# A decoder trunk on one core: low parts of 20 weight blocks formed by GpSimd and an adding transfer in place of VectorE

## The chip, the cores and the metric

The kernel runs on one core of one Trainium2 chip. The metric is the device time of one execution in microseconds. Before the change it was 1330.85 us, the median of three runs (1329.75 to 1331.48).

## The reference

The reference is a trunk of two layers on a sequence of 512 tokens with 1024 features, all in float32. Each layer does the following, cut to what matters here:

```
h = rms_norm(x) * (1 + sc_m) + sh_m
proj = h @ w_in          # 1024 x 3520
x_lru, q_down, kv_down, k_rope, gate_a, gate_b = split(proj)
y_a = rg_lru(conv(x_lru), ...)
y_b = mla(q_down, kv_down, k_rope, ...)        # 8 heads, causal
y = sigmoid(gate_a) * y_a + sigmoid(gate_b) * y_b
x = x + g_m * (y @ w_out)
h = rms_norm(x) * (1 + sc_f) + sh_f
x = x + g_f * ((silu(h @ w_gate) * (h @ w_up)) @ w_ffn_out)
```

The modulation columns sc, sh and g come from a product of the conditioning vector with w_ada (1024 x 6144 in each layer). A last rms_norm ends the trunk.

## The kernel before, in words

Activations lie feature-major: a tile is 128 features by 512 tokens. Each product is made in float32r with operands cut in two: a high part (the value rounded by a copy into float32r) and a low part (value minus high part). Of the four partial products three are made, hi x hi, hi x lo and lo x hi (mm3), so a weight block of 128 output features and 1024 input features takes 24 matmuls of 512 columns: in each group of three, the third one reads the low part of the weight (mm<-hh,wlo).

A weight block is fetched and cut by w_cols. SyncE issues a load of 512 KB into a raw tile; ScalarE copies raw into the tile whi; VectorE subtracts whi from raw into wlo. There are three raw tiles (NRAW) and three pairs of whi and wlo (NHL), which all weights of the kernel share. A raw tile is free again once the low part exists; a pair is free again once the block's 24 matmuls have read it. With dma=True, as before in the last layer's second FFN product alone (fo_block), the low part is made in another way: ScalarE copies whi with scale -1 into wlo, and GpSimd issues a transfer that adds raw to wlo in place.

The first layer begins with first_products, which streams two parts of w_ada and 960 columns of w_in together (x0 to x3 and the down projections). The other 20 blocks of the first layer's w_in go through w_cols: four of x_lru (x4 to x7, called in x_lru through product) and eight each of the two gates (called in gate). The mixer's steps of each layer are listed in SCRIPT: convolution, gates, decay and recurrence of the RG-LRU (x, g, e, w), rope, pairs, scores, transposes and values of the attention (r, p, q, s, t, v), the gates a and b, the merge y, and m, a background step that loads 512 KB of w_ada into a graw tile and reduces it on VectorE. The rotated parts of the queries are put together by 64 small transfers to the tiles stk, issued by SyncE.

No instruction is issued in this textual order. The Recorder collects all calls, and Recorder.order plans them: for each engine it picks the ready call with the longest tail, with modelled durations, modelled latencies between engines, and the limits of the tile pools. Each engine then works through its own list strictly in order. For a transfer issued by GpSimd the plan assumes POOL_DMA ns of issue and POOL_LAT ns more until the data is there; SyncE's loads have constants of their own.

Of the kernel before, what the change touches and what calls it, by code (L numbers as in the profile page):

```python
# [16 lines left out]
AF = mybir.ActivationFunctionType  # L17
ALU = mybir.AluOpType
# [3 lines left out]
P = 128  # L22
# [3 lines left out]
KD = D // P  # L26
# [6 lines left out]
NF = D_FF // P  # L33
# [33 lines left out]
H0, H1, FULL = slice(0, 256), slice(256, 512), slice(0, 512)  # L67
# [38 lines left out]
DMA_RUN = 0.6  # L106
DMA_LAT = 2400.0
DMA_ISSUE = 470.0
POOL_DMA = 1200.0
POOL_LAT = 6000.0  # L110
SHORT = 2000.0
TABLE_LOAD = 1300.0
PE_WINDOW = 3413.0
# [81 lines left out]
class Recorder:  # L195
# [77 lines left out]
    def cost(self, op, eng, method, a, k, outs, ins):  # L273
# [30 lines left out]
        if eng == "POOL":  # L304
            if method == "dma_start":
                return POOL_DMA
            if method == "tensor_scalar":
# [7 lines left out]
    def order(self):  # L315
# [98 lines left out]
        while count < n:  # L414
            for e in ENGINES:
# [62 lines left out]
                end = now + d  # L478
                if e == "POOL" and o.dur == POOL_DMA:
                    end += POOL_LAT  # L480
                if e == "SP":
# [56 lines left out]
def trunk(  # L538
# [7 lines left out]
    V, A, T, G, DMA = (  # L546
        rec.engine(e, r)
        for e, r in (("DVE", nc.vector), ("ACT", nc.scalar), ("PE", nc.tensor), ("POOL", nc.gpsimd), ("SP", nc.sync))
    )
# [12 lines left out]
    def unit(s, dt=F32):  # L562
        return rec.tile(up, [P, 512], dt, "u", NU, nm(s))

    def psum(tag):
        return rec.tile(pp, [P, 512], F32, "ps", BANKS["ps"], nm(tag))
# [7 lines left out]
    def f(ap):  # L574
        return ap.bitcast(F32)

    def split(hi, lo, src):
        A.activation(hi, src, AF.Copy)
        V.tensor_tensor(lo, src, f(hi), ALU.subtract)
# [6 lines left out]
    def mm3(ps, wh, wl, xh, xl, start, stop, **k):  # L586
        T.matmul(ps, wh, xh, start=start, stop=False, **k)
        T.matmul(ps, wh, xl, start=False, stop=False, **k)
        T.matmul(ps, wl, xh, start=False, stop=stop, **k)


    def raw_tile():
        return rec.tile(wp, [P, 1024], F32, "raw", NRAW, nm("raw"))

    def hl_tiles():
        return (
            rec.tile(wp, [P, 1024], F32R, "whi", NHL, nm("whi")),
            rec.tile(wp, [P, 1024], F32R, "wlo", NHL, nm("wlo")),
        )
# [6 lines left out]
            res.append((hi, lo))  # L606
        return res

    def w_cols(src, nk=KD, raws=None, dma=False):


        raw = raw_tile()
        DMA.dma_start(raw[:, : nk * P], src)
        hi, lo = hl_tiles()
        if dma:
            A.activation(hi[:, : nk * P], raw[:, : nk * P], AF.Copy)
            A.activation(lo[:, : nk * P], f(hi[:, : nk * P]), AF.Copy, scale=-1.0)
            G.dma_start(f(lo[:, : nk * P]), raw[:, : nk * P], accum_op=ALU.add)
        else:
            split(hi[:, : nk * P], lo[:, : nk * P], raw[:, : nk * P])  # L620
        if raws is not None:
            raws.extend(raw[:, k * P : (k + 1) * P] for k in range(nk))
        return [(hi[:, k * P : (k + 1) * P], lo[:, k * P : (k + 1) * P]) for k in range(nk)]
# [61 lines left out]
    for i in range(2):  # L685
        ps, crow, cs = psum("pt"), unit("crow"), slice(i * 512, (i + 1) * 512)
# [152 lines left out]
    class Ahead:  # L839
# [12 lines left out]
        def units(self, srcs):  # L852

            raws, res = [], []
            for src in srcs:
                raws.append([])
                w = w_cols(src, raws=raws[-1])
                ps = psum("mm")
                for k, (wh, wl) in enumerate(w):
                    mm3(ps, wh, wl, *self.t[k], k == 0, k == KD - 1)  # L860
                res.append(ps)
            pb, col = psum("o"), small(2 * max(1, NAHEAD), "shc")
            for i in range(len(srcs)):
                a, b = unit("wsa"), unit("wsb")
                for k in range(KD):
                    t = (a if k < 4 else b)[:, (k % 4) * P : (k % 4 + 1) * P]
                    G.tensor_scalar(t, raws[i][k], mcol(self.l, self.ssh, k), 1.0, ALU.mult, ALU.mult)
                G.tensor_tensor(a, a, b, ALU.add)
                G.tensor_tensor(a[:, : 2 * P], a[:, : 2 * P], a[:, 2 * P :], ALU.add)
                G.tensor_tensor(a[:, :P], a[:, :P], a[:, P : 2 * P], ALU.add)  # L870
                T.matmul(pb[:, i : i + 1], a[:, :P], ones[:, :1], start=True, stop=True)
            V.tensor_copy(col[:, : len(srcs)], pb[:, : len(srcs)])
            return res, [col[:, i : i + 1] for i in range(len(srcs))]


    def w_quarters(srcs):

        raws = []
        for src in srcs:
            raw = raw_tile()  # L880
            DMA.dma_start(raw, src)
            raws.append(raw)
        lo_, hi_ = slice(0, 512), slice(512, 1024)
        a11, a12, a21, a22 = raws[0][:, lo_], raws[0][:, hi_], raws[1][:, lo_], raws[1][:, hi_]
        s1, s2, s3, s4 = (unit("ws") for _ in range(4))
        res = {}
        h, l_ = hl_tiles()
        split(h, l_, raws[0])
        res["A11"], res["A12"] = (h[:, lo_], l_[:, lo_]), (h[:, hi_], l_[:, hi_])

        def add(name, s):
            res[name] = unit("wsh", F32R), unit("wsl", F32R)
            split(*res[name], s)

        V.tensor_tensor(s1, a21, a22, ALU.add)
        V.tensor_tensor(s2, s1, a11, ALU.subtract)
        add("S2", s2)
        V.tensor_tensor(s3, a11, a21, ALU.subtract)
        add("S3", s3)
        add("S1", s1)  # L900
        add("A22", a22)
        V.tensor_tensor(s4, a12, s2, ALU.subtract)
        add("S4", s4)
        return res
# [30 lines left out]
    def gemm_units(units, xh, xl, get_w, done):  # L935

        ws = {}
        for m, cs in units:
            if m not in ws:
                ws[m] = get_w(m)  # L940
            w = ws[m]
            ps = psum("mm")
            for k, (wh, wl) in enumerate(w):
                mm3(ps[:, cs], wh, wl, xh[k][:, cs], xl[k][:, cs], k == 0, k == len(w) - 1)
            done(m, cs, ps)
            bg()
# [102 lines left out]
    def layer(l, rs, ahead):  # L1049
        last = l == L - 1  # L1050
# [6 lines left out]
        def product(w):  # L1057
            ps = psum("mm")
            for k, (wh, wl) in enumerate(w):
                mm3(ps, wh, wl, hh[k], hl[k], k == 0, k == KD - 1)  # L1060
            return ps
# [9 lines left out]
        if l == 0:  # L1071
            for m in range(3):
                done_down(m, FULL, accs[4 + m])
            ps = accs[NFIRST]
        else:
# [7 lines left out]
            ps = psum("mm")  # L1083
# [30 lines left out]
        xi, v, av, lru_w = {}, {}, {}, {}  # L1114
# [7 lines left out]
        def conv(n, ps):  # L1122
            xc = unit("xc")
            A.activation(xc, ps, AF.Identity, bias=col2(R_CB, n), scale=cw(3, n))
            for i in (2, 1, 0):
                d = 3 - i
                V.scalar_tensor_tensor(xc[:, d:], ps[:, : S - d], cw(i, n), xc[:, d:], ALU.mult, ALU.add)
            xch, xcl = unit("xch", F32R), unit("xcl", F32R)
            split(xch, xcl, xc)
            return xc, xch, xcl  # L1130
# [37 lines left out]
        def x_lru(n):  # L1168
            if l == 0 and n < 4:
                ps = unit("xl")  # L1170
                A.activation(ps, accs[n], AF.Copy)
            else:
                ps = product(w_cols(w_in[l, n]))
            convs[n] = conv(n, ps)


# [117 lines left out]
        prs, pts, pos, sas, sbs, yhl = {}, {}, {}, {}, {}, {}  # L1294

        def gate(h, off, res):
            ps = product(w_cols(w_in[l, off + h]))
            res[h] = unit("sg")
            A.activation(res[h], ps, AF.Tanh, scale=0.5)
            if off == OFF_GA:  # L1300
                V.tensor_scalar(res[h], res[h], 1.0, None, ALU.add)

        def merge(h):
# [10 lines left out]
            "s": lambda h: prs.__setitem__(h, scores(h)), "t": lambda h: pts.__setitem__(h, transposes(prs.pop(h))),  # L1314
            "v": lambda h: pos.__setitem__(h, values(h, pts.pop(h))),
            "a": lambda h: gate(h, OFF_GA, sas), "b": lambda h: gate(h, OFF_GB, sbs),
            "y": merge, "m": bg, "d": down_sums, "n": down_norm,
        }
        for word in SCRIPT[l].split():
            steps[word[0]](int(word[1:]))  # L1320
        yh, yl = [yhl[h][0] for h in range(NH)], [yhl[h][1] for h in range(NH)]
# [7 lines left out]
        def done_out(m, cs, ps):  # L1329
# [2 lines left out]
            ahead.add(m, cs)  # L1332

        gemm_units(
            [(m, FULL) for m in range(KD)], yh, yl, lambda m: w_cols(w_out[l, m]), done_out,
        )


# [77 lines left out]
            split(ah[fi], al[fi], g)  # L1416

        def w_fi_cols(m):
            return w_cols(w_fi[l, m // 2 + (m % 2) * NF])

        def residual(m, cs, ps):
            V.scalar_tensor_tensor(x[m][:, cs], ps[:, cs], mcol(l, G_F, m), x[m][:, cs], ALU.mult, ALU.add)
# [54 lines left out]
        def fo_block(tiles, ms, done):  # L1477

            k0, nk = tiles[0], len(tiles)
            gemm_units(  # L1480
                ms, [ah[i] for i in tiles], [al[i] for i in tiles],
                lambda m: w_cols(w_fo[l, m, :, k0 * P : (k0 + nk) * P], nk, dma=last), done,
            )


# [22 lines left out]
    for l in range(L):  # L1508
        r = layer(l, *r)
# [51 lines left out]
```

## Time and profile before

| | |
|---|---|
| median of three runs | 1330.85 us |
| the profiled execution | 1330.39 us |
| its span, first to last instruction | 1328.6 us |
| TensorE busy | 1309.8 us (99%) |
| VectorE busy | 945.7 us (71%) |
| ScalarE busy | 676.2 us (51%) |
| GpSimd busy | 235.1 us (18%) |
| granted TensorE clock, mean | 0.998 |

PE is TensorE's matmuls, PEld its weight loads, DVE is VectorE, ACT ScalarE, POOL GpSimd, and SPq the queue of SyncE. Busy time leaves out register, semaphore and DMA-issuing instructions. A wait is put down to the instruction that ended it. Times count from the span's start, in us; the mean duration of a group's instructions is in ns. Nearly all instructions have one line number, since the planner issues them from one place, so groups are told apart by the names of their tiles: raw, whi and wlo for weights, graw for w_ada, sc for the softmax, kl and vl for low parts of keys and values.

### The profile page before, as it was taken

The page shows a single profiled execution, that of the slowest core. Times are in us where ns is not written, and L with a number is a line of the kernel's source. Part 1 is how long each engine was busy: PE and PEld are TensorE (multiplying, and loading weights), DVE is VectorE, ACT ScalarE, POOL GpSimd, SP SyncE. Part 2 cuts the span into 40 slices and gives each one's busy share as a digit, 9 for nine tenths or more (in the row PEclk, how much of TensorE's full clock was granted, in tenths as well). Part 3 has the DMA queues.
Part 4 walks back from the last instruction along what each step waited for, and adds up shares of the span by engine and source line. Part 5 has one row for each costly group of instructions (what it writes and reads, how often), then busy time and mean ns, then how long its engine had stood idle before and what let it go on. Part 6 is the DMA issues. An engine that isn't in the chain of part 4 may idle for free.

```text
span 1328.6 us, 18151 instructions
## 1 busy us (share of the span) xinstructions
PE 1309.8 (99%) x6788; PEld 1119.4 (84%) x6788; DVE 945.7 (71%) x1625; ACT 676.2 (51%) x1057; POOL 235.1 (18%) x250
## 2 busy tenths in 40 slices
PE   9999999999999999999999999999999999999997
PEld 7787878888888888888888888888888999899986
DVE  7999887897755555555679886666687766667634
ACT  4597676635322222222356867855474544444532
POOL 0414534314000000000211433312400000000011
PEclk9999999999999999999999999999999999999999
DMA  8744344172655555555414231211333444544473
GB/s 291 237 121 152 117 127 143 64 229 104 220 177 181 172 209 176 183 206 172 147 59 149 94 115 64 96 48 48 106 101 109 133 118 135 155 129 134 126 157 109
DMA packets 56012, 186.44 MB, mean 140 GB/s; under 512 B 7026, under 2 KB 7282, under 8 KB 55924
## 3 DMA queue, kind: packets, MB, share of 16 engines
q1 hardware_dynamic: 52468, 173.75, 39.6%
q0 software_dynamic: 3456, 11.54, 4.7%
q8 instruction: 53, 0.87, 0.3%
q14 instruction: 35, 0.29, 0.1%
HBM read 167.44 MB, written 2.10 MB: 128 GB/s over the span
## 4 chain that ended last, share of the span: by engine, by line
PE 88%; DMA 4%; ACT 3%; DVE 2%; SPq 1%; issue 1%; POOL 0%; DVEq 0%; ACTq 0%
PE mm L524 78%; PE s L524 4%; PE o L524 2%; PE pt L524 2%; DMA raw<-in_w_in_dram 1%; DMA raw<-in_w_ada_dram 1%; SPq L524 1%; DMA graw<-in_w_ada_dram 1%; ACT whi L524 1%; ACT L524 0%; DMA raw<-in_w_ffn_in_dram 0%; DVE raw L524 0%; DMA raw<-in_w_first_dram 0%; DMA crow<-in_c_dram 0%; ACT xc L524 0%
## 5 line engine op out<-in xcount | busy, mean ns | idle before, releaser
L524 ACT ACTIVATE whi<-raw 128x1024 fp32r<-128x1024 f32 (+2 forms) x192 | 199.3, 1038 | 434.6 <-PE mm L524 318.1
L524 DVE TENSOR_TENSOR wlo<-raw,whi 128x1024 fp32r<-128x1024 f32 (+1 forms) x167 | 206.9, 1240 | 103.9 <-ACT whi L524 99.9
L524 PE MATMUL mm<-hl,whi 128*128 128x512 f32 x432 | 168.9, 391 | 0.3 <-DVE hl L524 0.3
L524 PE MATMUL mm<-hh,whi 128*128 128x512 f32 x432 | 166.2, 394 | 1.8 <-ACT ri L524 1.4
L524 PE MATMUL mm<-hh,wlo 128*128 128x512 f32 x416 | 161.8, 390 | 0.0
L524 PE MATMUL mm<-al,whi 128*128 128x512 f32 (+1 forms) x360 | 139.1, 386 | 0.0
L524 PE MATMUL mm<-ah,whi 128*128 128x512 f32 (+1 forms) x360 | 138.9, 386 | 0.0
L524 PE MATMUL mm<-ah,wlo 128*128 128x512 f32 (+1 forms) x360 | 138.5, 385 | 0.0
L524 PE MATMUL mm<-fh,whi 128*128 128x512 f32 x336 | 130.5, 389 | 0.0
L524 PE MATMUL mm<-fh,wlo 128*128 128x512 f32 x336 | 130.5, 389 | 0.0
L524 PE MATMUL mm<-fl,whi 128*128 128x512 f32 x336 | 130.4, 389 | 0.0
L524 PEld LDWEIGHTS mm<-hh,whi 128*128 128x128 f32 x432 | 80.9, 188 | 19.0 <-ACT ri L524 1.5
L524 PEld LDWEIGHTS mm<-hl,whi 128*128 128x128 f32 x432 | 81.2, 188 | 17.4 <-DVE hl L524 1.4
L524 PEld LDWEIGHTS mm<-hh,wlo 128*128 128x128 f32 x416 | 78.1, 188 | 16.0
L524 PE MATMUL mm<-xqh,wsl 128*128 128x256 f32 x320 | 90.4, 283 | 0.0
L524 PE MATMUL mm<-xql,wsh 128*128 128x256 f32 x320 | 90.4, 283 | 0.0
L524 PE MATMUL mm<-xqh,wsh 128*128 128x256 f32 x320 | 90.4, 284 | 0.0
L524 DVE CUSTOM_DVE_ANT_0 graw<-graw,cb,cols 128x1024 f32<-128x1024 f32 x64 | 83.4, 1303 | 6.5 <-DMA graw<-in_w_ada_dram 5.7
L524 POOL TENSOR_SCALAR wsa<-raw,mod 128x128 f32<-128x128 f32 x24 | 17.2, 736 | 388.6 <-PE mm L524 339.4
L524 PEld LDWEIGHTS mm<-ah,whi 128*128 128x128 f32 x360 | 67.7, 188 | 13.2
L524 PEld LDWEIGHTS mm<-ah,wlo 128*128 128x128 f32 x360 | 67.7, 188 | 13.2
L524 PEld LDWEIGHTS mm<-al,whi 128*128 128x128 f32 x360 | 67.7, 188 | 12.6
(257 smaller groups left out, 3055.7 us busy)
## 6 DMA issues: line engine op xcount, KB each, us to landing
graw<-in_w_ada_dram SPq DMA_DIRECT2D x88, 512.0 KB, 4.5
raw<-in_w_ffn_in_dram SPq DMA_DIRECT2D x88, 512.0 KB, 3.4
raw<-in_w_in_dram SPq DMA_DIRECT2D x47, 512.0 KB, 3.4
raw<-in_w_ffn_out_dram SPq DMA_DIRECT2D x32, 448.0 KB, 3.5
raw<-in_w_out_dram SPq DMA_DIRECT2D x16, 512.0 KB, 3.4
raw<-in_w_ffn_out_dram SPq DMA_DIRECT2D x16, 512.0 KB, 3.9
wlo<-raw POOLq DMA_DIRECT2D x16, 448.0 KB, 4.4
raw<-in_w_ada_dram SPq DMA_DIRECT2D x8, 512.0 KB, 4.7
```

Of the source, the lines that this page charges most:

```text
L524: o.call(*(real(v) for v in o.a), **{k: real(v) for k, v in o.k.items()})
```

## The change

The option dma of w_cols becomes how, a letter for each place and layer, and the new function split_by makes the low part. "v" is the copy on ScalarE and the subtraction on VectorE, as before. "a" is the way that dma=True had. "g" differs from "a" in that GpSimd forms the negative high part by a multiplication with -1, and then issues the adding transfer. The letters are "g" for the first layer's w_in and "v" for the second's, "v" for w_out, for the first FFN product and for the blocks of w_quarters, and "v" and "a" for the second FFN product of the two layers, as it was. The planner's POOL_DMA goes from 1200 to 900 ns and POOL_LAT from 6000 to 3700 ns.

```diff
-POOL_DMA = 1200.0
-POOL_LAT = 6000.0
+
+HOW_IN = "gv"
+HOW_OUT = "vv"
+HOW_FI = "vv"
+HOW_FO = "va"
+HOW_A1 = "v"
+POOL_DMA = 900.0
+POOL_LAT = 3700.0
...
-    def w_cols(src, nk=KD, raws=None, dma=False):
+    def split_by(how, hi, lo, src):
+
+
+        if how == "v":
+            split(hi, lo, src)
+            return
+        A.activation(hi, src, AF.Copy)
+        if how == "a":
+            A.activation(lo, f(hi), AF.Copy, scale=-1.0)
+        else:
+            G.tensor_scalar(lo, f(hi), -1.0, 1.0, ALU.mult, ALU.mult)
+        G.dma_start(f(lo), src, accum_op=ALU.add)
+
+    def w_cols(src, nk=KD, raws=None, how="v"):
 
 
         raw = raw_tile()
         DMA.dma_start(raw[:, : nk * P], src)
         hi, lo = hl_tiles()
-        if dma:
-            A.activation(hi[:, : nk * P], raw[:, : nk * P], AF.Copy)
-            A.activation(lo[:, : nk * P], f(hi[:, : nk * P]), AF.Copy, scale=-1.0)
-            G.dma_start(f(lo[:, : nk * P]), raw[:, : nk * P], accum_op=ALU.add)
-        else:
-            split(hi[:, : nk * P], lo[:, : nk * P], raw[:, : nk * P])
+        split_by(how, hi[:, : nk * P], lo[:, : nk * P], raw[:, : nk * P])
...
-        split(h, l_, raws[0])
+        split_by(HOW_A1, h, l_, raws[0])
...
-                ps = product(w_cols(w_in[l, n]))
+                ps = product(w_cols(w_in[l, n], how=HOW_IN[l]))
...
-            ps = product(w_cols(w_in[l, off + h]))
+            ps = product(w_cols(w_in[l, off + h], how=HOW_IN[l]))
...
-                lambda m: w_cols(w_fo[l, m, :, k0 * P : (k0 + nk) * P], nk, dma=last), done,
+                lambda m: w_cols(w_fo[l, m, :, k0 * P : (k0 + nk) * P], nk, how=HOW_FO[l]), done,
```

The calls for w_out and the first FFN product get how=HOW_OUT[l] and how=HOW_FI[l] in the same way.

## Rows read from the trace of the kernel before

**Rows 1.** The page: busy us, share of the span and instructions of each engine.
```profile
PE 1309.8 (99%) x6788; PEld 1119.4 (84%) x6788; DVE 945.7 (71%) x1625; ACT 676.2 (51%) x1057; POOL 235.1 (18%) x250
```

**Rows 2.** Busy time by window, then clock, DMA share, GB/s; four windows of the first layer.
```profile
core 0: us, PE busy (x) PEld busy (x) DVE busy (x) ACT busy (x) POOL busy (x), PEclk, DMA share, GB/s
56.00:60.00 4.00, 3.70 (x16) 2.74 (x15) 3.56 (x5) 2.84 (x4) 3.57 (x7) 1.00 0.58 190
60.00:216.00 156.00, 149.32 (x729) 123.97 (x728) 143.01 (x269) 119.27 (x203) 63.35 (x57) 1.00 0.42 132
216.00:330.00 114.00, 114.00 (x579) 97.43 (x578) 93.60 (x175) 61.96 (x106) 41.42 (x43) 1.00 0.40 134
...
190.00:194.00 4.00, 3.16 (x17) 2.48 (x16) 4.00 (x7) 3.60 (x6) 1.34 (x1) 1.00 0.96 271
```

**Rows 3.** Waits of TensorE in 60 to 320 us: total us, times, longest.
```profile
PE mm L524 <- ACT ri L524: 1.4, 1, 1.4
...
PE s L524 <- DVE kl L524: 1.3, 1, 1.3
PE mm L524 <- DVE vl L524: 0.8, 1, 0.8
```

**Rows 4.** Chain of waits in 40 to 330 us: start us, us, what.
```profile
100.61 4.02 DMA raw<-in_w_in_dram
...
190.00 6.18 DMA raw<-in_w_in_dram
...
198.07 3.92 DMA graw<-in_w_ada_dram
```

**Rows 5.** Waits of SyncE's queue in 60 to 216 us: total us, times, longest.
```profile
SPq L524 <- DVE wlo L524: 48.8, 12, 8.4
```

**Rows 6.** Groups by form, VectorE, 60 to 320 us: busy us, mean ns, idle before.
```profile
L524 DVE TENSOR_TENSOR wlo<-raw,whi 128x1024 fp32r<-128x1024 f32 x30 | 40.3, 1343 | 7.0 <-ACT whi L524 6.5 <-PE pt L524 0.3
```

**Rows 7.** Groups by form, GpSimd, the whole span: busy us, mean ns, idle before.
```profile
L524 POOL DMA_DIRECT2D wlo<-raw x24 | 21.0, 875 | 322.8 <-ACT wlo L524 174.0 <-ACT pq L524 74.6 <-PE mm L524 60.2
...
L524 POOL TENSOR_SCALAR sc<-sc,sm 128x512 f32<-128x512 f32 x16 | 14.9, 929 | 73.7 <-DVE sm L524 55.5 <-PE o L524 12.7 <-issue 5.4
...
L524 POOL TENSOR_SCALAR sc<-sc,sm 128x128 f32<-128x128 f32 x16 | 11.3, 709 | 0.0
```

**Rows 8.** DMA queues and issues of the page; landing times of the tile wlo.
```profile
q0 software_dynamic: 3456, 11.54, 4.7%
...
wlo<-raw POOLq DMA_DIRECT2D x8, 512.0 KB, 4.8
...
DMA to landing us min/median/max: 4.2/4.6/7.9
```

**Rows 9.** Instructions in order of time, ScalarE and VectorE: start us, us, what.
```profile
56.05 1.06 ACT L524 ACTIVATE whi<-raw 128x1024 fp32r<-128x1024 f32 x1 [0.71 <-DMA raw<-in_w_in_dram]
78.81 1.05 ACT L524 ACTIVATE whi<-raw 128x1024 fp32r<-128x1024 f32 x1
85.73 1.07 ACT L524 ACTIVATE whi<-raw 128x1024 fp32r<-128x1024 f32 x1
...
224.96 1.06 ACT L524 ACTIVATE whi<-raw 128x1024 fp32r<-128x1024 f32 x1 [1.43 <-PE mm L524]
...
57.14 1.23 DVE L524 TENSOR_TENSOR wlo<-raw,whi 128x1024 fp32r<-128x1024 f32 x1
96.70 2.32 DVE L524 TENSOR_TENSOR wlo<-raw,whi 128x1024 fp32r<-128x1024 f32 x1
...
226.49 1.22 DVE L524 TENSOR_TENSOR wlo<-raw,whi 128x1024 fp32r<-128x1024 f32 x1
```

**Rows 10.** In order of time, TensorE and GpSimd: third matmuls, the last transfer.
```profile
62.05 0.39 PE L524 MATMUL mm<-hh,wlo 128*128 128x512 f32 x1
88.99 0.39 PE L524 MATMUL mm<-hh,wlo 128*128 128x512 f32 x1
...
1302.27 0.87 POOL L524 DMA_DIRECT2D wlo<-raw  x1 [5.04 <-ACT wlo L524]
...
1307.92 0.39 PE L524 MATMUL mm<-ah,wlo 128*128 128x512 f32 x1
```

More of the change, by code (lines that the diff above doesn't have):

```diff
@@ L1334, in layer @@
         gemm_units(
-            [(m, FULL) for m in range(KD)], yh, yl, lambda m: w_cols(w_out[l, m]), done_out,
+            [(m, FULL) for m in range(KD)], yh, yl, lambda m: w_cols(w_out[l, m], how=HOW_OUT[l]), done_out,
         )
@@ L1418, in w_fi_cols @@
         def w_fi_cols(m):
-            return w_cols(w_fi[l, m // 2 + (m % 2) * NF])
+            return w_cols(w_fi[l, m // 2 + (m % 2) * NF], how=HOW_FI[l])
         def residual(m, cs, ps):
```

## The prediction

> **What bounds the kernel now.** I read the busy table first: TensorE is busy 99% of the span and VectorE 71% [rows 1], so a change that leaves TensorE's work alone can only win where TensorE stands still. The table by windows then says where that is. In 60 to 216 us, where the first layer's mixer runs, TensorE is busy 149.32 of 156 us; in 216 to 330 us, where its last four input blocks and its output projection run, it never stops [rows 2]. So 6.7 us of visible standstill lie in the stage that the change touches; no gain there can exceed them by much. In the same 156 us VectorE is busy 143.0 us (92%), ScalarE 119.3 (76%), GpSimd 63.4 (41%), and the DMA engines 42% [rows 2]. VectorE is the fullest of TensorE's suppliers.
>
> The list of who waited for whom gives the standstill by cause: eight waits in 60 to 320 us, 6.6 us together. Three of them, 2.4 us, end with VectorE (kl 1.3 and vl 0.8 are shown, the third is 0.3); five, 4.2 us, end with ScalarE, the longest 1.4 [rows 3]. The chain of waits shows that "ended with" isn't the whole story: before the stop at 106 us stands a weight load issued at 100.61 (4.02 us), after it the copy whi and the activation ri queued behind that copy; before the stop at 206 us stand a load of 6.18 us, SyncE's queue, a load of w_ada of 3.92 us, and only then kl on VectorE [rows 4]. So the largest stops hang on loads. And the loads hang on VectorE in part: SyncE's queue stood 48.8 us in 12 waits for wlo, the subtraction that releases a raw tile [rows 5].
>
> **What goes.** The edit touches 20 blocks (x4 to x7, eight a and eight b gates of layer 0). In each, one VectorE subtraction 128x1024 goes. There are 30 such in 60 to 320 us at 1343 ns mean [rows 6], 19 of them of this edit. 20 x 1.34 = 26.9 us leave VectorE, 16 of them (21.5 us) inside 60 to 216 us: 143.0 falls to 121.5, 78% of 156.
>
> **What comes, on GpSimd.** 20 negations 128x1024 with one SBUF input. None is in the trace. Nearest: the softmax scaling, 709 ns for 128 columns and 929 ns for 512 [rows 7], so 0.573 ns a column and 929 + 512 x 0.573 = 1.22 us. Bounds: no less than 0.93 us, the same operation at half the size; no more than twice that, 1.86 us. I take 1.22 us, since it follows 32 measured rows of that operation. Then 20 transfer issues at 0.875 us [rows 7]. Sum 20 x (1.22 + 0.875) = 42 us, of which 16 x 2.1 = 33.5 us fall into 60 to 216 us: GpSimd is occupied 62% there in place of 41%.
>
> **What comes, on the DMA engines.** The 24 adding transfers of the last layer took 4.7% of 16 engines' span [rows 8], 62 us, so 2.6 us each. 16 more in 60 to 216 us add 42 us of 156: the share goes from 42% to 69%. That is room on average, but it was already 96% in 190 to 194 us [rows 2], where TensorE stood.
>
> **What moves: when a low part is ready.** Before, the subtraction ended 3.6 us after the copy whi in the mean over the 20 blocks (of the 20 pairs of rows the first and the last are shown, 1.3 and 1.7 us); the two worst, in VectorE's backlog, took 12.2 and 14.3 us, the first of them copied at 85.73 and subtracted at 96.70 to 99.02 [rows 9]. Now it is 0.1 us of semaphore, 1.22 of negation and 4.8 from issue to landing for 512 KB [rows 8], 6.1 us; bounds 5.2 (0.93 and the fastest landing, 4.2) and 9.9 (1.86 and the slowest, 7.9) [rows 8]. TensorE needs a low part at a block's third matmul. Measured so, with the order of before: block 1 is copied by 57.11 and would land at 63.2, but TensorE wants it at 62.05 [rows 9, 10]: 1.2 us late. Block 4 is copied by 79.86, lands at 86.0, is wanted at 88.99 [rows 9, 10]: 3.0 us to spare. All the others have between 3.8 us and 28 us. So one block in 20 costs something. At that place nothing covers it: the first products end at 61.6, and what comes next needs their results through ScalarE. GpSimd's polynomial for the table column is busy 3.57 of 4 us there [rows 2], so the negation may wait up to one such operation, 1.2 us, more: 1.2 to 2.4 us late, 6.2 by the upper bound (9.9 in place of 6.1). I take 1.3, near the lower end, since the planner places the operation that TensorE's chain needs first.
>
> The new constants (900 and 3700 ns in place of 1200 and 6000) also shape the order of the last layer, whose 24 transfers stay as they are. There TensorE's last blocks take up their low parts about 0.8 us after they land: issued at 1302.27, landing 4.8 us later, wanted at 1307.92 [rows 10]. Their start is set by the release of the hl tiles, not by the planned latency, so I cost this at zero; by those rows it could gain 1 us or lose 2. If the cover of 0.8 us goes, each of the last six blocks pays what is missing.
>
> **The sum.** The profiled execution took 1330.39 us, 1328.6 of them the span; the median of the timed runs is 1330.85, 0.46 higher. From it: the three VectorE-ended stops go, -2.4 (that of kl, behind loads, because the raw tiles ahead of them are not kept by VectorE's backlog). Of the ScalarE-ended 4.2 us, I let two thirds go, -2.8: raw tiles in the backlog come free earlier (the one copied at 85.73 at about 93 in place of 99.02), so the load behind the stop at 106 us can be issued before the row of small stk transfers rather than behind it; the remaining third is what ScalarE itself sets, for it is full in 60 to 90 us. Block 1 costs +1.3. Together -3.9: 1330.39 - 3.9 + 0.46 = 1327.0 us. What is late next is ScalarE, then SyncE's queue. The ends: all 6.7 us and the 2 to 3 us of small gaps that the busy table doesn't count give 1330.85 - 9.5 = 1321; nothing gained and block 1 at its upper end gives 1337.
>
> **A rule that speaks against it.** A subtraction wlo that overlaps a GpSimd operation took 2.32 us (at 96.70) against 1.23 us alone [rows 9]. The Trainium skill ("SBUF — State Buffer", "Who interferes with whom") says that a VectorE instruction with two SBUF inputs contends with a GpSimd instruction that reads SBUF, and that the loser fully blocks for the whole instruction. The row agrees. That gives the first rival.
>
> **Rivals.** (1) *VectorE is held by the negations, no change.* Each negation stops VectorE for its own length wherever a two-input instruction is due: up to 20 x 1.22 = 24.4 us given back out of 26.9. For it: the 2.32 us row, and the many two-input operations on VectorE. Against it: some of VectorE's time goes to inputs in PSUM, and a GpSimd operation can fall into a gap. Then no stop goes, block 1 costs 1.3: 1330.85 + 1.3 = 1332.
>
> (2) *The raw tiles are held longer and SyncE's queue jams, slower.* A raw tile is now released by the landing, 6.1 us after the copy in place of 3.6 in the mean. SyncE issues in order with three raw tiles, so behind a load that waits stand the stk transfers that the scores need and the w_ada loads that VectorE waits for. For it: the 48.8 us of such waits, and the DMA share at 190 us. Against it: most raw tiles are waiting for an hl tile, not for VectorE. If the three stops that hang on loads (106, 198 and 206 us) each grow by 2.5 us, block 1 costs 1.3 and the other stops stay, 1330.85 + 7.5 + 1.3 = 1339.6; with the 2.4 us of VectorE's gain kept, 1337. It decides once the time from copy to low part passes about 9 us (6.1 plus the 3.0 us of block 4), which a landing like the slowest measured, 7.9 us, reaches.
>
> (3) *The edit does nothing on VectorE's account*: if the order rather than VectorE's load sets the stops, the new order's own stops replace them, between -2 and +2 us. I count it with (1).
>
> **How the numbers follow.** Forecast 0.42, own range 1321 to 1328; (1) with (3) 0.30, 1328.2 to 1333.5; (2) 0.28, 1333.5 to 1341. A difference under 0.2% (2.7 us) can't be told from no change here. The range 1320.5 to 1337.5 leaves out 0.03 below and about 0.13 above.
>
> **What would show it.** VectorE's wlo group falls by 20 and its busy time by about 27 us, less if (1) holds: then the mean of its two-input operations rises. GpSimd shows 20 negations near 1.2 us, 44 transfer issues, busy near 260 us in the page's count, which leaves issues out. TensorE is seen waiting for a transfer near 62 us, 1 to 2.4 us. The stops at 192 and 206 us are gone; if rather the waits of SyncE for wlo transfers exceed 49 us and TensorE stands over 8 us in 60 to 216 us, (2) was right. The forecast is wrong if TensorE's busy share of that stage doesn't rise.

## The result: 1.3% slower, all of it in the first layer's mixer

The changed kernel took 1350.15 us (median of four runs, 1347.37 to 1352.87), the kernel before 1331.16 beside it: a ratio of 1.0135, 95% interval 1.0108 to 1.0163. I had forecast 1327.0 with a range up to 1337.5, so sign and range were both wrong. The profiled execution took 1352.87 us. Its page answers to [rows 1]:

```profile
PE 1320.4 (98%) x6788; PEld 1125.7 (83%) x6788; DVE 935.5 (69%) x1605; ACT 686.4 (51%) x1065; POOL 266.1 (20%) x290
```

TensorE has the same 6788 matmuls and is busy 10.6 us longer. To find where, I cut both executions at the same two instructions: the end of the first products, and the fourth matmul of the output projection. Between them lies the mixer, with the same 1037 matmuls on either side. The columns are those of [rows 2]; first the kernel before (start-up, mixer, rest), then the changed one, with one short window more.

```profile
0.00:61.37 61.37, 58.47 (x291) 46.12 (x292) 50.94 (x94) 27.61 (x40) 9.64 (x20) 1.00 0.82 279
61.37:272.27 210.90, 204.22 (x1037) 172.33 (x1036) 185.81 (x369) 152.28 (x268) 83.48 (x75) 1.00 0.38 123
272.27:1328.60 1056.33, 1047.07 (x5462) 900.95 (x5460) 708.92 (x1164) 496.35 (x752) 142.01 (x156) 1.00 0.44 136
```

```profile
0.00:66.00 66.00, 61.59 (x291) 47.63 (x292) 51.12 (x94) 27.86 (x40) 9.95 (x20) 0.95 0.74 254
66.00:294.88 228.88, 211.90 (x1037) 177.33 (x1036) 174.10 (x349) 162.61 (x275) 114.89 (x116) 0.96 0.60 161
294.88:1350.40 1055.52, 1046.93 (x5462) 900.77 (x5460) 710.31 (x1164) 495.90 (x752) 141.28 (x156) 1.00 0.42 136
134.80:138.00 3.20, 3.19 (x8) 2.56 (x9) 3.20 (x5) 3.17 (x6) 1.65 (x2) 0.55 0.50 170
```

- The mixer grew from 210.9 to 228.9 us, by 18.0. That is the whole difference of the medians, 19.0, to within a microsecond.
- Of it 10.3 us are standstill: length less busy time was 6.7 us and is 17.0. The other 7.7 us are the same matmuls taking longer (204.2 to 211.9), at a granted clock of 0.96 in place of 1.00. After a stop of 4.27 us the clock of the next 3.2 us was 0.55, so mostly at the lower level, 1.2 GHz. It was 0.50 in four stretches of the mixer (69.4 to 72.8, 134.3 to 137.6, 195.7 to 199.1 and 219.6 to 226.4 us), which lie beside the four longest stops, of 2.43, 4.27, 1.77 and 3.60 us.
- All that follows the mixer takes 0.8 us less. Nothing was lost or won in the last layer.
- Start-up is 4.6 us longer. It runs the same instructions in both kernels, and in the runs below it took 60.3 to 65.2 us whichever kernel it was, so I don't count it to the change.

Who was waited for, in the mixer (total us, times, longest), answers to [rows 3], the first fence TensorE, the second SyncE's queue [rows 5]; the line behind it is SyncE's of the kernel before over its own whole mixer:

```profile
PE s L530 <- DVE kl L530: 4.3, 1, 4.3
PE o L530 <- ACT ph L530: 3.6, 1, 3.6
PE mm L530 <- DMA wlo<-raw: 2.4, 1, 2.4
PE pt L530 <- ACT rwh L530: 1.8, 1, 1.8
PE mm L530 <- ACT sg L530: 1.6, 1, 1.6
PE s L530 <- ACT kh L530: 1.4, 1, 1.4
```

```profile
SPq L530 <- DMA wlo<-raw: 112.5, 16, 14.2
SPq L530 <- DVE wlo L530: 30.3, 3, 16.9
```

```profile
SPq L524 <- DVE wlo L524: 100.3, 17, 16.9
```

One wait of TensorE ends with an adding transfer, at block 1. The others end with ScalarE (8.4 us), VectorE (5.8 us) and, for 0.2 us, GpSimd; before it was ScalarE for 4.2 us and VectorE for 2.4 us. What stands before the longest is told by the chain of waits (start, us, what), then by TensorE's instructions around its end:

```profile
118.15 1.05 POOL wlo L530
...
119.56 6.67 DMA wlo<-raw
...
126.28 0.33 SPq L530
...
126.71 4.07 DMA graw<-in_w_ada_dram
...
130.92 2.12 DVE graw L530
...
134.15 0.61 DVE kl L530
```

```profile
134.81 0.79 PE L530 MATMUL s<-xch,lwh 128*128 128x512 f32 x1 [4.27 <-DVE kl L530]
...
136.25 0.63 PE L530 MATMUL mm<-hh,whi 128*128 128x512 f32 x1
136.68 0.63 PE L530 MATMUL mm<-hl,whi 128*128 128x512 f32 x1
...
138.30 0.39 PE L530 MATMUL mm<-hh,whi 128*128 128x512 f32 x1
138.53 0.39 PE L530 MATMUL mm<-hl,whi 128*128 128x512 f32 x1
```

VectorE's last two reductions of w_ada before it:

```profile
126.25 1.42 DVE L530 CUSTOM_DVE_ANT_0 graw<-graw,cb,cols 128x1024 f32<-128x1024 f32 x1
...
130.92 3.22 DVE L530 CUSTOM_DVE_ANT_0 graw<-graw,cb,cols 128x1024 f32<-128x1024 f32 x1 [3.24 <-DMA graw<-in_w_ada_dram]
```

Read from the top: GpSimd issues an adding transfer; it lands 6.67 us later; only then is a raw tile free and SyncE goes on in its queue to a load of w_ada; VectorE has to reduce that, and behind the reduction in its queue stands kl, for which TensorE waits. The stop costs 4.27 us, and after it matmuls start every 0.43 us in place of 0.23 until 137.5 us. The reduction itself took 3.22 us where the one before it took 1.42, while GpSimd's operations on a and ri ran beside it (129.91 to 133.06 us). By these two rows some 1.8 us of the stop are VectorE held, an estimate; the rest is the wait for the load.

The chains before the next stops are others. The one of 3.60 us (at 220.28) ends with small stk transfers, the last of which landed after 3.62 us; the one of 1.77 us (at 194.21) comes through GpSimd's own queue, where a negation stands ahead of ri; the one of 1.63 us (at 182.60) through VectorE's queue and a table load of ScalarE.

```profile
187.82 2.08 POOL wlo L530
...
193.52 0.64 ACT rwh L530
...
215.91 3.62 DMA stk<-oh
```

### The profile page after: what moved, and what is told of

It is laid out like the page before. It is cut to its first block, busy times and chain, and to the rows that moved or that the text cites. A ratio compares the mean times of both kernels' runs of the same rounds, so it can differ in the third digit from the quotient of the medians.

```text
span 1350.4 us, 18222 instructions
## 1 busy us (share of the span) xinstructions
PE 1320.4 (98%) x6788; PEld 1125.7 (83%) x6788; DVE 935.5 (69%) x1605; ACT 686.4 (51%) x1065; POOL 266.1 (20%) x290
## 4 chain that ended last, share of the span: by engine, by line
PE 85%; issue 7%; DMA 3%; DVE 3%; POOL 2%; ACT 1%; SPq 0%; DVEq 0%; POOLq 0%; ACTq 0%
PE mm L530 76%; PE s L530 4%; PE o L530 3%; PE pt L530 2%; DMA raw<-in_w_in_dram 1%; DMA wlo<-raw 1%; POOL wlo L530 1%; POOL ri L530 1%; DVE t L530 0%; POOL w L530 0%; POOL sc L530 0%; DMA raw<-in_w_ffn_in_dram 0%; DMA graw<-in_w_ada_dram 0%; DMA stk<-oh 0%; DVE sc L530 0%
## 5 line engine op out<-in xcount | busy, mean ns | idle before, releaser
L530 DVE TENSOR_TENSOR wlo<-raw,whi 128x1024 fp32r<-128x1024 f32 (+1 forms) x147 | 180.2, 1227 | 101.7 <-ACT whi L530 98.1
L530 POOL DMA_DIRECT2D wlo<-raw x44 | 39.0, 893 | 327.3 <-ACT wlo L530 199.7
L530 DVE CUSTOM_DVE_ANT_0 graw<-graw,cb,cols 128x1024 f32<-128x1024 f32 x64 | 87.4, 1368 | 6.5 <-DMA graw<-in_w_ada_dram 6.3
```

Source lines behind the costliest of these rows:

```text
L530: o.call(*(real(v) for v in o.a), **{k: real(v) for k, v in o.k.items()})
```

## The experiments

The planner makes a new order whenever a duration or an operation changes. So the question was how much of the loss is the new *order*, and how much the *mechanism* (negation and transfer) within an order. In some kernels the order is therefore held: an operation is planned as one thing and issued as another, by a field swap, a list of calls that are issued in its place (empty: nothing). The cost in us of a kernel is its ratio less one, times 1331; the change's is +18.0 (14.4 to 21.7).

### The order

**The order of the changed kernel, the work of the kernel before.** On VectorE the subtraction stands where the transfer was planned.

```diff
             G.tensor_scalar(lo, f(hi), -1.0, 1.0, ALU.mult, ALU.mult)
+            rec.ops[-1].swap = []
         G.dma_start(f(lo), src, accum_op=ALU.add)
+        if how == "g":
+            rec.ops[-1].swap = [(nc.vector.tensor_tensor, (lo, src, f(hi), ALU.subtract), {})]
```

> Every engine keeps the order of the changed kernel, but where GpSimd would issue the adding transfer of one of the 20 blocks, VectorE makes the subtraction instead, and the negation is left out. Theory L (the low part comes late, raw tiles are held to the landing, SyncE's queue jams): without the transfer the mixer's loss of 18 us goes, 1329 to 1335 us, and SyncE's waits on low parts fall from 103 us in 60 to 238 us to about 50. Theory P (the new order itself is worse: it has 8 more table loads on ScalarE and another order of matmuls): the loss stays, 1345 to 1350 us. In between, about 1340, each has half.

1339.38 us, ratio 1.0062 (1.0040 to 1.0084): +8.3 us. No transfer, no negation, no work more, and yet close to half of the loss. As both kernels issue the same matmuls in the same order, the stops can be compared one by one. That of 4.27 us is gone and that of 3.60 is 0.95, so the mechanism makes the one and most of the other; those of 1.63 and 1.77 are still 1.64 and 1.29, and others of up to 1.79 us came. One thing limits the number: the order was planned for a VectorE without the 20 subtractions, so the 8.3 us contain their unplanned places as well. The mixer took 219.25 us:

```profile
63.26:282.51 219.25, 208.08 (x1037) 173.43 (x1036) 184.09 (x368) 162.81 (x276) 78.99 (x72) 0.98 0.37 120
```

**The order of the kernel before, the mechanism of the changed one.** The planner's constants are the old ones here.

```diff
+        if how == "g":
+            split(hi, lo, src)
+            rec.ops[-1].swap = [
+                (nc.gpsimd.tensor_scalar, (lo, f(hi), -1.0, 1.0, ALU.mult, ALU.mult), {}),
+                (nc.gpsimd.dma_start, (f(lo), src), {"accum_op": ALU.add}),
+            ]
+            return
```

> Every engine keeps the order of the kernel before (planned with VectorE's subtraction and the old constants), but at the subtraction's place GpSimd makes the negation and issues the adding transfer. Theory L: the latency hurts in this order too, and more, since it wasn't planned for: 1345 to 1355 us, block 1 late by some 1 to 3 us, SyncE's waits over 90 us. Theory P: the order of before is good with either way, 1330 to 1335 us.

1361.96 us, 1.0227 (1.0192 to 1.0263): +30.2 us, the worst way to make the change. This is the kernel that my prediction in effect worked out, with the order of before and each block's margin, and for which it found one block in 20 late. TensorE waited for a transfer once there too, 1.4 us. But one stop for ri took 7.68 us, and one for kl 5.76. In the kernel before the same two matmuls stood 1.37 us and nothing, and one that waits for ph stood 1.34 us where it is 4.46 now. The row of the first; then the chain before the second, and its row:

```profile
120.81 0.79 PE L532 MATMUL mm<-hh,whi 128*128 128x512 f32 x1 [7.68 <-ACT ri L532]
```

```profile
245.82 1.72 POOL wlo L532
247.94 6.24 DMA wlo<-raw
254.62 7.80 DMA graw<-in_w_ada_dram
...
265.57 0.70 DVE kl L532
```

```profile
266.32 0.80 PE L532 MATMUL s<-kl,qh 128*128 128x512 f32 x1 [5.76 <-DVE kl L532]
```

It is the same path as at 134.81 us of the changed kernel: the landing that frees a raw tile, a load of w_ada behind it, VectorE, TensorE. Before the stop for ri stands a weight load that was issued behind the row of stk transfers and landed 7.34 us later, before 4.02 us [rows 4].

**Other orders with the work of before.** The planner is told that the 20 subtractions (letter j) take 0.1 us more, or 1 us more, with its old constants; and, separately, the new constants alone.

```diff
-        if how == "v":
+        if how in "vj":
             split(hi, lo, src)
+            if how == "j":
+                rec.ops[-1].dur += 100.0      # the other kernel: 1000.0
```

> The kernel before, all by VectorE, with one planner number changed: the 20 subtractions are planned 0.1 us longer. The first layer's order then differs from early on in every queue; the work is the same. If the order of before is a good find that any other order loses: 1334 to 1340 us. If only an order planned around a long latency is worse: 1328 to 1332 us.

> The kernel before with the 20 subtractions planned 1 us longer; the work is unchanged, the order is another one, with 7 table loads more on ScalarE (the changed kernel has 8 more). If an order planned around later low parts is in itself worse, as the order of the changed kernel by 8 to 10 us: 1337 to 1342 us. If only that one order was unlucky, or bad because it counts on a relieved VectorE: 1329 to 1334 us.

```diff
-HOW_IN = "gv"
+HOW_IN = "vv"
```

> The new planner constants with all 20 blocks made by VectorE as before. The order differs from that of before in the last layer's final FFN part only. All theories: within 2 us of the kernel before, 1329 to 1333 us. If the constants were the loss, 1345 or more.

With 0.1 us more, the order differs widely and the time doesn't: 1331.37, 1.0001 (0.9984 to 1.0019). With 1 us more it is 1339.04, 1.0059 (1.0042 to 1.0075), the loss of the first experiment again. The constants alone: 1331.56, 1.0013 (0.9995 to 1.0031), nothing. So in these runs a new order as such was free, and the two made for low parts that come later were not. The second of them was planned with VectorE's subtractions in place, which speaks for the order rather than for the unplanned places as the cause of most of the 8.3 us. A mark of these orders is ScalarE's table loads in the mixer, here before and after (busy us, mean ns):

```profile
L524 ACT ACT_TABLE_LOAD x20 | 25.7, 1283 | 1.6 <-PE mm L524 1.3
```

```profile
L530 ACT ACT_TABLE_LOAD x28 | 35.9, 1283 | 0.5
```

The order that lost 8.3 us has 28 as well, that of 1 us more 27, that of 0.1 us more 23. That the loads cause the loss was not shown: no run took them away alone.

### VectorE's relief

**ScalarE negates in place of GpSimd** (its own order).

```diff
-HOW_IN = "gv"
+HOW_IN = "av"
```

> As the changed kernel, but the negative high part of the 20 blocks is made by ScalarE, and planned so; GpSimd only issues the transfers. Theory Q: GpSimd's queue loses 24 us of work and its waits on whi, so part of the 19 us comes back, 1338 to 1345 us, unless ScalarE, which gets 20 us more, is full at 60 to 90 us. Theory L (lateness of the low part): no better than the changed kernel, 1348 to 1354 us.

1350.24 us, 1.0133 (1.0100 to 1.0166), as slow as the change. GpSimd is out of VectorE's way, and VectorE is relieved as far as I had thought it would be, 162.18 us of mixer in place of 185.81, but ScalarE rises from 152.28 to 178.50:

```profile
65.16:292.97 227.81, 209.04 (x1038) 176.29 (x1036) 162.18 (x349) 178.50 (x294) 89.51 (x95) 0.97 0.60 162
```

**Two blocks only**, the fifth and sixth of the 20 in the order of issue (the two whose subtractions came 12.2 and 14.3 us after the copy), in the order of before. A counter picks them as the operations are issued.

```diff
+                    nth += 1
+                    if nth in (5, 6):
+                        o.swap = o.other      # the list of the second experiment
```

> The order of the kernel before; only the fifth and the sixth of the 20 blocks, whose subtraction stood 12 and 14 us behind the copy in VectorE's backlog, get GpSimd's negation and the adding transfer. Both are then earlier than before, GpSimd stood idle there, and VectorE has 2.5 us less to do in its fullest stretch. Theory Q and L: no loss, 1328 to 1331 us, a gain of up to 2 us. If any transfer by GpSimd hurts: 2 to 3 us slower than before.

1334.60 us, 1.0017 (1.0001 to 1.0034). Nothing is won at the two places where VectorE's backlog was longest; at best nothing is lost.

**GpSimd subtracts, no transfer** (its own order).

```diff
-            G.tensor_scalar(lo, f(hi), -1.0, 1.0, ALU.mult, ALU.mult)
+            G.tensor_tensor(lo, src, f(hi), ALU.subtract)
+            return
```

> GpSimd makes the low part of the 20 blocks by one subtraction with two inputs (raw minus high part) and no transfer; the planner is told so. A low part is then there about 2.5 to 3 us after the copy, in place of 6. Theory L: little is lost, 1329 to 1336 us, for raw tiles come free nearly as early as before. Rival (GpSimd is too full, or its reads hold VectorE): 1340 us or more, with the mean of VectorE's two-input operations longer. If the DMA engines' load was the cause: as L.

1345.15 us, 1.0107 (1.0084 to 1.0130). A subtraction takes GpSimd 2.73 us, and VectorE's mixer is 194.1 us busy though 20 of its own are gone: it is held rather than relieved.

### The parts of the load

In the changed kernel's order, with VectorE subtracting as in the first experiment, single parts of the new load were added as dummies. They write a scratch tile, and to make room one of 72 small tiles (128x512) goes: the plan still counts 72, the kernel has 71. The control has this and one negation only.

```diff
-        return rec.tile(up, [P, 512], dt, "u", NU, nm(s))
+        r = rec.tile(up, [P, 512], dt, "u", NU - 1, nm(s))
+        rec.caps["u"] = NU
+        return r
...
+            rec.ops[-1].swap = [(nc.gpsimd.tensor_scalar, (d, f(hi), -1.0, 1.0, ALU.mult, ALU.mult), {})] if n_spare[0] == 20 else []
```

> The control for the runs with added negations, memsets and transfers: the same order, low parts by VectorE, the scratch tile and 71 units in place of 72 as there, but only one of the 20 negations is made. If the added work was what cost 8 to 13 us there: 1339 to 1341 us, as the order alone. If the one unit less was it: 1346 us or more, and the added work cost only the rest.

> The order of the changed kernel with low parts by VectorE (1339 without anything else), and GpSimd makes the 20 negations into a scratch tile that nothing reads; no transfers, no waits between negations. Theory Q (GpSimd works in order: each negation waits for its copy whi, and then occupies the queue in which the RG-LRU's and the softmax's operations stand): 1347 to 1355 us. Theory B (the transfers' DMA load): 1338 to 1342 us.

Control: 1348.06, 1.0119 (1.0095 to 1.0143). It spoils the easy reading of the others: one small tile less, with the scratch tile in its place and one negation, costs 7.6 us over the first experiment by itself. With all 20 negations (the last condition left out): 1352.87, 1.0166 (1.0137 to 1.0195), some 6 us over the control, the intervals just overlapping. What they do is seen on VectorE, whose mixer rises from 185.63 us busy in the control to 197.90, and whose 22 subtractions in it rise from 1336 ns to 1475; first the control, then the 20 negations:

```profile
63.23:288.53 225.30, 207.37 (x1037) 174.26 (x1036) 185.63 (x367) 162.40 (x274) 81.84 (x74) 0.98 0.36 116
L532 DVE TENSOR_TENSOR wlo<-raw,whi 128x1024 fp32r<-128x1024 f32 x22 | 29.4, 1336 | 1.9 <-ACT whi L532 1.9
```

```profile
61.60:292.54 230.94, 211.49 (x1037) 177.57 (x1036) 197.90 (x369) 162.65 (x275) 108.73 (x98) 0.96 0.35 114
L532 DVE TENSOR_TENSOR wlo<-raw,whi 128x1024 fp32r<-128x1024 f32 x22 | 32.5, 1475 | 1.9 <-ACT whi L532 1.9
```

Three other parts, each alone, 20 times: a memset where the negation was, an adding transfer of half the size from a constant tile, and one of 8 columns.

```diff
+            rec.ops[-1].swap = [(nc.gpsimd.memset, (f(d), 0.0), {})]
...
+                (nc.gpsimd.dma_start, (f(d), cb[:, :512]), {"accum_op": ALU.add}),
...
+                (nc.gpsimd.dma_start, (f(d[:, :8]), cb[:, :8]), {"accum_op": ALU.add}),
```

> As the run with the negations alone (1352.9), but in each negation's place GpSimd fills the scratch tile with a constant: its queue is occupied for a like time, but it reads nothing and doesn't wait for the copy whi. If GpSimd's queue is what costs: 1347 us or more. If what costs is that VectorE is held while GpSimd reads (VectorE's busy time in the mixer rose by 14 us with the negations): 1338 to 1343 us, VectorE busy as in the order alone, 184 us.

> The same order with low parts by VectorE, and GpSimd issues the 20 adding transfers, of half size, from a constant tile into two scratch tiles that nothing reads; no negations. Theory Q: only the issues count, 0.9 us each: 1340 to 1345 us. Theory B: half of what the DMA load costs, 1345 us or more, with loads landing later than their 3.4 us.

> As the run with the transfers alone (1350.1), but each of the 20 moves 8 columns in place of 512: GpSimd issues as much, the DMA engines move next to nothing. If the issues in GpSimd's queue are what costs: 1347 to 1351 us. If the DMA load does: 1338 to 1343 us.

Memsets of 963 ns: 1351.16, 1.0147 (1.0125 to 1.0170), with VectorE's mixer at 186.0 us against the control's 185.6, so without holding it. Half transfers: 1350.11, 1.0142 (1.0113 to 1.0171). Tiny ones: 1347.64, 1.0131 (1.0108 to 1.0154). None of the three can be told from the control; the issue alone costs nothing that shows.

**Negation and transfer in full as dummies**, the transfer once from a constant tile, once from raw, which is then held as in the change.

```diff
+            rec.ops[-1].swap = [(nc.gpsimd.tensor_scalar, (d, f(hi), -1.0, 1.0, ALU.mult, ALU.mult), {})]
...
+                (nc.vector.tensor_tensor, (lo, src, f(hi), ALU.subtract), {}),
+                (nc.gpsimd.dma_start, (f(d), cb), {"accum_op": ALU.add}),      # the other kernel: src for cb
```

> The order of the changed kernel, low parts by VectorE as in the run that keeps that order (1339). In addition GpSimd makes the 20 negations into a scratch tile and issues the 20 adding transfers from a constant tile into it, which nothing reads: GpSimd's and the DMA engines' load is there, but no low part is late and no raw tile is held. Theory L (lateness and held tiles): 1338 to 1342 us. Theory B (DMA share and GpSimd's queue): 1347 us or more. The scratch tile makes some negations wait for the transfer before.

> As the run with transfers from a constant tile, but the scratch transfers read the raw tile, so each raw tile is held until a landing while the low part itself is there early. If the held raw tile is what costs (SyncE's queue): 1346 to 1351 us. If the lateness of the low part at TensorE is what costs: as the run without held tiles, 1338 to 1342 us.

1365.19 (1364.62 to 1365.97) and 1369.33 us (1366.90 to 1372.23). As sizes of the change these say little, since GpSimd waited 23.4 and 24.8 us for the one scratch tile, which no part of the change does. Their difference counts: holding raw until the transfer has read it costs 4.1 us in the medians. The runs of the two don't overlap; the intervals of their ratios do (1.0217 to 1.0269 and 1.0250 to 1.0303).

**A fourth raw tile** in the changed kernel's order, again with 71 small tiles.

```diff
-        return rec.tile(wp, [P, 1024], F32, "raw", NRAW, nm("raw"))
+        r = rec.tile(wp, [P, 1024], F32, "raw", NRAW + 1, nm("raw"))
+        rec.caps["raw"] = NRAW
+        return r
...
```

> The changed kernel with its order unchanged, but with four raw tiles in memory (and 71 of the 72 units), so that SyncE's loads need not wait for the landing of the low part two blocks before. If the held raw tiles cost 10 us, 1339 to 1343 us, and SyncE's waits for wlo transfers fall from 112 us in 60 to 300 us to under 40. If the low part's lateness or GpSimd's load costs it, 1348 to 1352 us.

1351.52, 1.0145 (1.0121 to 1.0169): no gain. SyncE's waits for the transfers were 97.8 us in the mixer, where I had expected under 40, so in this order the fourth tile hardly relieves the queue. But a small tile less costs 7.6 us in the order of the first experiment, so this doesn't show that the fourth tile is worth nothing.

### A planner that knows

The same 20 transfers, planned with two things that the planner didn't know: a GpSimd operation that reads SBUF excludes VectorE's two-input operations, and a transfer needs 0.6 us longer to land.

```diff
-POOL_LAT = 3700.0
+POOL_LAT = 4300.0
...
+        if eng == "POOL" and method != "dma_start" and any(isinstance(x, Ref) and x.shape[-1] > 1 for x in ins):
+            op.shared = True
```

> The changed kernel, but the planner is told more of what the runs showed: GpSimd's reads of one input and VectorE's operations of two inputs exclude each other, and a transfer lands 4300 ns after its issue in place of 3700. If the loss comes from a plan that doesn't know these: 1335 to 1343 us. If there is no room for the added work in any order: 1346 to 1352 us.

> The planner with the added knowledge of VectorE and GpSimd, and all low parts by VectorE as in the kernel before. If the knowledge is worth more than the adding transfers cost: below the kernel before, 1324 to 1329 us. If the order of before was already as good: 1329 to 1335 us; any other order loses up to 8 us, as those planned later did.

1339.30 us, 1.0061 (1.0043 to 1.0079): over half of the loss is gone with the same work. The second has this planner and HOW_IN = "vv", VectorE subtracting: 1332.36, 1.0009 (0.9994 to 1.0024), the kernel before again. So in the orders of this planner the mechanism costs about 7 us, and what the planner didn't know some 10 us more. The mixer of the first:

```profile
64.25:280.75 216.50, 207.41 (x1037) 174.95 (x1036) 171.82 (x350) 156.95 (x271) 116.74 (x118) 0.98 0.63 170
```

No version beat the kernel before.

## Why the prediction was wrong, step by step

**The bound: right, and it should have ruled.** I read that the stage held 6.7 us of standstill, so that no gain there could be large. ScalarE's negations show that the bound went further: with VectorE at 162 us in place of 186, though with the transfers and an order of its own, TensorE stood 18.8 us in place of 6.7. The two gains of my sum, -2.4 and -2.8 us, didn't come: the stops that end with VectorE and ScalarE grew from 2.4 and 4.2 us to 5.8 and 8.4. My test of the forecast, a rising busy share of TensorE in the stage, came out against it, at 93% of the mixer in place of 97%. VectorE was the fullest supplier, yet in the chains shown here it was the last link and not the first.

**What goes: mis-sized.** 20 subtractions left VectorE (x1625 to x1605), but its busy time fell by 10.2 us of the page and not by 26.9. That negations hold VectorE, as rival 1 had it, is shown by the dummies: 185.63 us of mixer in the control, 197.90 with 20 negations. How much of the rest came back that way in the changed kernel is not shown. VectorE's reduction of w_ada in the mixer, before and after:

```profile
L524 DVE CUSTOM_DVE_ANT_0 graw<-graw,cb,cols 128x1024 f32<-128x1024 f32 x8 | 11.6, 1451 | 0.0
```

```profile
L530 DVE CUSTOM_DVE_ANT_0 graw<-graw,cb,cols 128x1024 f32<-128x1024 f32 x8 | 15.7, 1957 | 3.2 <-DMA graw<-in_w_ada_dram 3.2
```

With ScalarE negating, the same group took 1392 ns. It also differs between orders without the 20 negations (1337 ns in the control, 1784 with subtractions planned 1 us longer), so this group alone doesn't tell what held it. The rule named in the prediction (the Trainium skill, "SBUF — State Buffer", "Who interferes with whom") is borne out by the negation dummies and by the memsets: what writes only did not hold VectorE (186.03 us).

**What comes: right in its sizes.** Predicted were a negation of 1.22 us, issues of 0.875, landings of 4.8 and a DMA share of 69%; GpSimd's two groups and the landings of the tile (min, median, max) were:

```profile
L530 POOL TENSOR_SCALAR wlo<-whi 128x1024 fp32r<-128x1024 f32 x20 | 24.5, 1226 | 33.8 <-ACT whi L530 33.7
L530 POOL DMA_DIRECT2D wlo<-raw x20 | 18.1, 921 | 4.5 <-POOL wlo L530 4.0 <-PE mm L530 0.4
```

```profile
DMA to landing us min/median/max: 4.5/5.0/8.7
```

The share was 0.60 in the mixer. GpSimd's busy time came to 266.1 us for about 260; that the page leaves the issues out was wrong (x250 to x290).

**When a low part is ready: mis-sized.** I had 6.1 us from the end of the copy to the landing. Over the 20 blocks it was 8.4 us in the mean (6.1 to 11.9) in the changed kernel, and 8.4 again in the order of before. In the changed kernel 0.8 us of that pass before the negation starts, 1.2 in it, 0.7 between its end and the issue, and 5.7 until the landing: I had taken a median where the mean counts, and no time in GpSimd's queue. Six blocks of the 20 took over 9 us in either kernel. An ordinary one is the block whose transfer starts the chain shown first above; its copy ended at 118.06 and the transfer landed at 126.23:

```profile
117.00 1.06 ACT L530 ACTIVATE whi<-raw 128x1024 fp32r<-128x1024 f32 x1 [4.63 <-DMA raw<-in_w_in_dram]
```

**Block 1: right.** I had 1.2 to 2.4 us late, taking 1.3; it was the upper end, as the negation began at 63.17, 1.9 us after the copy and behind three steps of the polynomial:

```profile
69.73 0.80 PE L530 MATMUL mm<-hh,wlo 128*128 128x512 f32 x1 [2.43 <-DMA wlo<-raw]
```

**The step that failed: "So one block in 20 costs something", and the sum built on it.** The count was right: TensorE waits for one transfer. What was wrong is to take that as the price. A low part that comes in time for TensorE may still come late for the raw tile, and the raw tile for SyncE's queue. In the order of before, where my margins were read, this cost 30.2 us against my 1.3. I had this as rival 2 and put its start at 9 us from copy to low part, which the forecast of 6.1 us kept away; with 8.4 us in the mean and six blocks past 9, it was there. Of the three stops that I let grow by 2.5 us each, in the order of before that at 106 us grew by 6.3 and that at 198 us by 3.1; the one at 206 us shrank to 0.3, and a new one of 5.76 us came. The chain of rival 2 stands before the longest stop of the changed kernel, and holding raw had its own price, 4.1 us.

**A second step, in rival 3: "the new order's own stops replace them, between -2 and +2 us".** I had put the order's price at nothing. With the work of before, the order of the changed kernel costs 8.3 us.

**A term that I left out: the clock.** I costed stops by their length. In the mixer 10.3 us of stops came with 7.7 us of slower matmuls, so a microsecond stopped cost 1.75 in this execution; in the control's, 11.3 us of stops more than before came with 3.1 us. Rival 2 at 7.5 us of stops would have been 13 by the first rate.

**The sign I named was no sign.** SyncE's waits for wlo transfers (112.5 us, over my 49) were to tell rival 2, together with a standstill of TensorE over 8 us, which came (17.0 us in the mixer). But SyncE waited 100.3 us for the subtractions over the mixer before, 105.5 in the first experiment, and 100.7 for transfers with the informed planner. The total doesn't tell whether a queue jams; only the chain before a stop does.

**The last layer and the constants: right**, at -0.8 us in the profile and +1.7 (-0.7 to +4.1).

**Open:** how the 9.7 us that the change costs beyond its order divide between held raw tiles, held VectorE, GpSimd's own queue and fuller DMA queues. The dummies showed 3 to 6 us each for held tiles, negations and transfers, with intervals about as wide, and the negations don't tell a held VectorE from a held queue. For a part of the last speak the landings in the mixer, here of w_ada and of the small stk transfers, before and after:

```profile
graw<-in_w_ada_dram SPq DMA_DIRECT2D x16, 512.0 KB, 4.4
stk<-oh SPq DMA_DIRECT2D x16, 64.0 KB, 2.0
```

```profile
graw<-in_w_ada_dram SPq DMA_DIRECT2D x16, 512.0 KB, 5.3
stk<-oh SPq DMA_DIRECT2D x16, 64.0 KB, 3.6
```

The loads of w_in went from 3.6 to 4.0 us. In the first experiment, the same order without transfers, w_ada took 5.0 us, w_in 3.8 and stk 2.0, so it is the stk transfers that the added ones slow most.

## What to carry over

Where a program plans the order, a changed latency is two changes; plan one kind of work and issue the other, to price them apart. Relieving the busiest supplier can gain only where the chain before a stop begins with it, and a buffer's release counts as a consumer beside the engine that needs the data. Every dummy needs a control that has its scratch and not its work.

## What I had not expected of the hardware

- The clock: at 0.55 for 3.2 us after a stop of 4.27 us, with matmuls of 512 columns 0.43 us apart in place of 0.23, and at 0.50 beside each of the four longest stops.
- Start-up of one and the same order ended between 60.3 and 66.0 us. In the profiled execution of the changed kernel the granted clock was 0.71 in 8 to 16 us.
- One small tile of 72 less, with a scratch tile in its place and one negation, cost 7.6 us (1.0119 against 1.0062), nearly as much as the order.
